# TensorE's order of the first layer written down: scan steps at fixed places among the dense products

## The chip, the cores and the metric

The kernel runs on one core of one Trainium2 chip. The metric is the device time of one launch in microseconds (us), smaller is better. The core's engines run side by side: TensorE (PE in the profile; its weight loads are PEld), VectorE (DVE), ScalarE (ACT), GpSimd (POOL) and SyncE (SP), which here issues nearly all DMAs. Each engine has its own list of instructions, works through it in order, and waits on semaphores where an input or a buffer isn't ready.

## The reference

A two-layer encoder trunk on x of shape (1, 512, 1024), float32. The first layer, the one that the change touches, is a Mamba-2 mixer:

```python
zxbcdt = rms_norm(x, norm_g) @ w_in                  # z 2048, x 2048, B 1024, C 1024, dt 32
xbc = silu(causal_depthwise_conv(xbc, conv_w, conv_b))
y = ssd_chunked_scan(xs * dt, a * dt, bm, cm)        # 8 groups of 4 heads of 64, state 128
y = gated_group_rms_norm(y + d_skip * xs, z, gate_norm_g)
x = x + y @ w_out
```

Of one chunk the scan computes, with `cb = C B^T` within the chunk, `y = (cb * decay) xdt + (C state) exp(acs)` and `state' = state exp(acs_end) + B^T (xdt to_end)`. The second layer is differential attention against one shared K/V projection, and a final RMSNorm follows. Both are outside the change.

## The kernel before

**Dense products.** Every large matrix is used as a high part and a low part (`whi`, `wlo` for weights, made on ScalarE and VectorE from the loaded `raw`), and a product of two such pairs is three TensorE products of 128x512 in a row (`mm3`); three such products are called a triple here. The dense work of the first layer is cut into items that run in the order `z0 g0 g1 z1 g2 g3 z2 g4 o0 g5 z3 g6 g7 o1 o2 o3`: `z` is a quarter of the gate's projection, `g` the projection of one group's B, C and x, `o` a quarter of the output projection (which needs the finished y of two groups). Each item is 32 triples, `o3` here 16 (its other half is done by `last_rows`). A generator, `stream_a`, yields after each triple. `z0` is done ahead of it.

**Scan steps.** When the dense products of group g are traced, `ssd(g)` traces that group's scan, whose TensorE parts are small float32 products and transposes. In the words of the trace and the code: `pcb` (C B^T), `pbt` (transpose of B), `pxt` (transpose of x, two halves), `psA` and `psB` (what the chunks add to the state, L605 to L613), `pyd` (products inside the chunks, 64 small ones, L618 to L625), `po1` and `po2` (C times the state, L633 to L637; `po<-hst` in the trace), and `pyt` (transposes of the normed y). Between them the other engines work: ScalarE copies the first state out of `psA` (L607), GpSimd decays it (L608), and VectorE adds the second half of `psA` to it (L609, `hst<-psA` in the trace). This addition is the last reader of `psA`.

**Buffers.** The eight PSUM banks go by tag: four `mm` for dense products, three `ss`, one `long`. Of a group the `ss` tiles are taken in the order pbt, pxt, pxt, psA, psB, pyd half 0, po1, po2, pyt, pyt. While `psA`, `psB` and `pyd` half 0 are held, none is left, and `po1` takes the bank of whichever is given back first.

**What sets the order.** The program is traced through Tile, which reorders: when the program is built, a list scheduler plays it against a timing model (`schedule_with_timeline_sim=True`) and so fixes each engine's list. An instruction traced earlier has the higher priority; the weights' splitting and the last group's `ssd(7)` have a raised one. `Ordered` wraps the engines: while its `on` is set, an instruction is pinned behind the one traced before it on that engine. In the first layer it is set on TensorE from `psA` to `pyd` (L604 to L626); all else there is where the scheduler's model put it. In `o3` the low and high parts of y of groups 6 (inner steps k = 0, 1) and 7 (k = 2, 3) are used. The splitting of the weights for `last_rows` is pinned on VectorE behind `root_end`, the last instruction of the latest reciprocal root (L273).

Of the kernel before, what the change touches and what calls it, by code (L numbers as in the profile page):

```python
# [13 lines left out]
ALU = mybir.AluOpType  # L14
# [6 lines left out]
NT = S // P  # L21
KD = D // P
G = 8
# [13 lines left out]
BLOCKS = [(it, k) for it in ORDER_B if it[0] not in "bc" for k in range(2 if it[0] == "v" else 1)]  # L37


C_GA, C_GK, C_GB, C_GG, C_SG, C_DTB, C_AL, C_CB, C_CW = 0, 8, 16, 24, 40, 41, 42, 43, 75  # L40
N_PAR = 203

# [3 lines left out]
class Ordered:  # L46


    def __init__(self, tc, engine):
        self.tc, self.engine, self.on = tc, engine, False  # L50

    def __getattr__(self, name):
        op = getattr(self.engine, name)

        def call(*args, **kw):
            i = op(*args, **kw)  # L56
            if self.on:
                self.tc.keep_in_program_order(i)
            return i

        return call
# [3 lines left out]
def trunk(ctx, tc, x, x_t, par, w_dt, w_in, w_out, w_kvqg, w_bo, d_skip, lam_qk, fin_g, out):  # L65
    nc = tc.nc
    V, A, T = (Ordered(tc, e) for e in (nc.vector, nc.scalar, nc.tensor))
# [8 lines left out]
    def mm_bank(name):  # L76
        return psum.tile([P, 512], F32, tag="mm", name=name, bufs=4)
# [4 lines left out]
    def ss_bank(name):  # L82
        turns[0] += 1
        tag = "mm" if turns[0] % turns[1] >= 3 else "ss"
        return psum.tile([P, 512], F32, tag=tag, name=name, bufs=3 if tag == "ss" else 4)

    def long_bank(name):
        return psum.tile([P, 512], F32, tag="long", name=name)
# [13 lines left out]
    x_tok = res.tile([P, NT, D], F32, name="x_tok")  # L102
# [142 lines left out]
    def mm3(ps, lhs, rhs, first, last, **kw):  # L245
        (lh, ll), (rh, rl) = lhs, rhs
        T.matmul(ps, lhsT=lh, rhs=rh, start=first, stop=False, **kw)
        T.matmul(ps, lhsT=lh, rhs=rl, start=False, stop=False, **kw)
        T.matmul(ps, lhsT=ll, rhs=rh, start=False, stop=last, **kw)

    root_end = [None]

    def rsqrt(v, n, tag, bufs=2):


        y = small.tile([P, n], F32, tag=f"{tag}_y", name=f"{tag}_y", bufs=bufs)
        c = small.tile([P, n], F32, tag=f"{tag}_c", name=f"{tag}_c", bufs=bufs)
        iy = small.tile([P, n], I32, tag=f"{tag}_i", name=f"{tag}_i", bufs=bufs)

        def vyy():  # L260
            if n == 1:
                V.scalar_tensor_tensor(out=c, in0=y, scalar=v, in1=y, op0=ALU.mult, op1=ALU.mult)
            else:
                V.tensor_tensor(out=c, in0=y, in1=v, op=ALU.mult)
                V.tensor_tensor(out=c, in0=c, in1=y, op=ALU.mult)

        V.tensor_scalar(out=iy, in0=v.bitcast(I32), scalar1=1, scalar2=None, op0=ALU.logical_shift_right)
        V.tensor_scalar(out=y.bitcast(I32), in0=iy, scalar1=-1.0, scalar2=float(0x5F3759DF - 2 ** 31), op0=ALU.mult, op1=ALU.add)
        vyy()
        V.scalar_tensor_tensor(out=c, in0=c, scalar=-10.0 / 3.0, in1=c, op0=ALU.add, op1=ALU.mult)  # L270
        V.scalar_tensor_tensor(out=y, in0=c, scalar=5.0, in1=y, op0=ALU.add, op1=ALU.mult)
        vyy()
        root_end[0] = V.scalar_tensor_tensor(out=y, in0=c, scalar=-64.0 / 3.0, in1=y, op0=ALU.add, op1=ALU.mult)  # L273
        return y
# [20 lines left out]
    dense = [None]  # L295
# [5 lines left out]
    def until(key):  # L301
        while key not in done:
            next(dense[0], None)
# [76 lines left out]
    xt = [bp2.tile([P, 2, S], F32, tag="yl", name=f"xt{i}", bufs=4) for i in range(4)]  # L380
# [136 lines left out]
                    outs.append(conv(pg[i], *fts[i]))  # L517
        conv_out[g] = outs

    def out_mm(po, j, t, w):  # L520
        tk = slice(t * P, (t + 1) * P)
        for k in range(4):
            yh, yl = yT[2 * j + k // 2]
            mm3(po, (yh[:, k % 2, tk], yl[:, k % 2, tk]), (w[0][:, k, :], w[1][:, k, :]), k == 0, k == 3)
            yield

    def out_proj(j):
        for n in range(2 if j < 3 else 1):
            w = (use if j < 3 else use_b)(("o", j, n))
            ns = slice(n * 512, (n + 1) * 512)  # L530
            for t in range(NT):
                po = mm_bank(f"po{j}_{n}_{t}")
                yield from out_mm(po, j, t, w)
                V.tensor_tensor(out=x_tok[:, t, ns], in0=po, in1=x_tok[:, t, ns], op=ALU.add)
                if j == 3:
                    sq = small.tile([P, S], F32, tag="wide", name=f"sq3_{t}", bufs=2)
                    A.activation(sq, x_tok[:, t, ns], AF.Square, accum_out=bss[:, 0, t:t + 1])

    def stream_a():
        for it in order_a[1:]:  # L540
            j = int(it[1])
            yield from {"z": z_proj, "g": group_proj, "o": out_proj}[it[0]](j)
            done.add(it)
        while True:
            yield

    bss = small.tile([P, 2, NT], F32, name="bss", bufs=1)
    decs = {}
# [20 lines left out]
    def ssd(g):  # L569
        bc, cc, x0, x1 = conv_out.pop(g)  # L570
        xc = (x0, x1)
        dec, een, _ = decs.pop(g)
        hs = slice(R * g, R * g + R)

        pcb = long_bank(f"pcb{g}")
        for c in range(NQ):
            cs = slice(c * P, (c + 1) * P)
            T.matmul(pcb[:, cs], lhsT=bc[:, cs], rhs=cc[:, cs], start=True, stop=True)
        pbt = ss_bank(f"pbt{g}")
        for c in range(3):  # L580
            T.transpose(pbt[:, c * P:(c + 1) * P], bc[:, c * P:(c + 1) * P], ident)
        bt = bp.tile([P, 3, P], F32, tag="bt", name=f"bt{g}")
        A.copy(bt.rearrange("p c n -> p (c n)"), pbt[:, 0:3 * P])
        xdt = bp.tile([P, NQ, R, HD], F32, tag="xdt", name=f"xdt{g}")
        dx = bp.tile([P, NQ, R, HD], F32, tag="dx", name=f"dx{g}")
        for j in range(2):
            pxt = ss_bank(f"pxt{g}_{j}")
            for c in range(NQ):
                T.transpose(pxt[:, c * P:(c + 1) * P], xc[j][:, c * P:(c + 1) * P], ident)
            pv = pxt.rearrange("p (c h e) -> p c h e", h=2, e=HD)  # L590
            h2 = slice(R * g + 2 * j, R * g + 2 * j + 2)
            V.tensor_tensor(out=xdt[:, :, 2 * j:2 * j + 2, :], in0=pv, in1=dt_tok[:, :, h2].unsqueeze(3).to_broadcast([P, NQ, 2, HD]), op=ALU.mult)
            V.tensor_tensor(out=dx[:, :, 2 * j:2 * j + 2, :], in0=pv,
                            in1=dsk[:, h2].unsqueeze(1).unsqueeze(3).to_broadcast([P, NQ, 2, HD]), op=ALU.mult)
# [6 lines left out]
        hst = bp.tile([P, 3, R, HD], F32, tag="hst", name=f"hst{g}")  # L601
        hsf = hst.rearrange("p c h e -> p c (h e)")
        psA = ss_bank(f"psA{g}")
        T.on = True  # L604
        for c in range(2):  # L605
            T.matmul(psA[:, c * 256:(c + 1) * 256], lhsT=bt[:, c, :], rhs=xe[:, c].rearrange("p h e -> p (h e)"), start=True, stop=True)
        A.copy(hsf[:, 0], psA[:, 0:256])  # L607
# [11 lines left out]
        for q in (1, 0):  # L619
            for c in (2 * q, 2 * q + 1):  # L620
                for h in reversed(range(R)):
                    o = (c % 2) * 256 + h * HD

                    for r in (slice(0, 64), slice(64, 128)):
                        T.matmul(pyd[q][r, o:o + HD], lhsT=dec[:, h, c, r], rhs=xdt[:, c, h, :], start=True, stop=True)  # L625
        T.on = False  # L626
        for q in range(2):
            dq = dx[:, 2 * q:2 * q + 2].rearrange("p c h e -> p c (h e)")
            V.tensor_tensor(out=dq, in0=pyd[q].rearrange("p (c e) -> p c e", c=2), in1=dq, op=ALU.add)
# [2 lines left out]

        po1 = ss_bank(f"po1{g}")  # L633
        T.matmul(po1[:, 256:512], lhsT=cc[:, P:2 * P], rhs=hsf[:, 0], start=True, stop=True)
        po2 = ss_bank(f"po2{g}")
        for c in (2, 3):
            T.matmul(po2[:, (c - 2) * 256:(c - 1) * 256], lhsT=cc[:, c * P:(c + 1) * P], rhs=hsf[:, c - 1], start=True, stop=True)  # L637
        V.tensor_tensor(out=tmp[:, 1], in0=po1[:, 256:512].rearrange("p (h e) -> p h e", e=HD),
                        in1=eacs_tok[:, 1, hs].unsqueeze(2).to_broadcast([P, R, HD]), op=ALU.mult)
        V.tensor_tensor(out=tmp[:, 2:4], in0=po2.rearrange("p (c h e) -> p c h e", h=R, e=HD),  # L640
                        in1=eacs_tok[:, 2:4, hs].unsqueeze(3).to_broadcast([P, 2, R, HD]), op=ALU.mult)
        u = dx.rearrange("p c h e -> p c (h e)")
        tm = tmp.rearrange("p c h e -> p c (h e)")
# [7 lines left out]
        r4 = rsqrt(v4, NQ, "y")  # L651
        for c in range(NQ):
            if g == G - 1 and c % 2:
                V.tensor_scalar(out=tm[:, c], in0=u[:, c], scalar1=r4[:, c:c + 1], scalar2=None, op0=ALU.mult)
            else:
                A.activation(tm[:, c], u[:, c], AF.Copy, scale=r4[:, c:c + 1])
        yh = bp2.tile([P, 2, S], F32R, tag="yh", name=f"yh{g}", bufs=4)
# [2 lines left out]

        n = 2 if g == G - 1 else NQ
        for j, a in [(j, a) for a in range(0, NQ, n) for j in range(2)]:
            for c in range(a, a + n):
                T.transpose(pyt[j][:, c * P:(c + 1) * P], tm[:, c, j * P:(j + 1) * P], ident)
            cs = slice(a * P, (a + n) * P)
            A.copy(yh[:, j, cs], pyt[j][:, cs])
            V.tensor_tensor(out=yl[:, j, cs], in0=pyt[j][:, cs], in1=yh[:, j, cs].bitcast(F32), op=ALU.subtract)
        yT[g] = (yh, yl)

    decays((0, 1))  # L670
    dense[0] = stream_a()
    for g in range(G):
        until(f"g{g}")
        if g < G - 1:
            ssd(g)
        else:
            with tc.high_priority():
                ssd(g)
    until("o3")


    hh, hl = new_h("b")
# [27 lines left out]
    due = [0.0]  # L710
# [98 lines left out]
    st = {}  # L809
# [157 lines left out]
    def half(t, n):  # L967
        hs = slice(n * 512, (n + 1) * 512)
        return x_tok[:, t, hs], fg[:, hs], ot[t][:, hs], out[t * P:(t + 1) * P, hs]
# [123 lines left out]
    y, f, o, dst = half(3, 0)  # L1093
# [8 lines left out]
    y, f, o, dst = half(3, 1)  # L1102
# [68 lines left out]
```

## Time and profile before

| | |
|---|---|
| median of 3 runs | 708.0 us (707.85 to 708.36) |
| profiled execution, its own time | 707.88 us |
| its span, first to last instruction | 706.1 us, granted TensorE clock 0.997 |
| busy: PE / PEld / DVE / ACT / POOL | 696.0 / 580.3 / 516.9 / 426.5 / 111.8 us |
| first layer's part touched by the change | about 45 us to 410 us of the span |

How to read it: a row of the timeline has start and duration in us, engine, line, operation, output and inputs by the program's names, shape and count; a bracket at its end is idle time of the engine ahead of it and who ended it. Nearly every instruction goes through the wrapper and so stands under L56, hence groups are told apart by tiles. TensorE products are pipelined: a product of 128x512 is shown as 0.39 us long, but the next one starts about 0.23 us after it, so start-to-start times are what counts.

### The profile page before, as it was taken

To read this page: it belongs to the slowest core of one execution; us is meant where nothing else is said; L and a number is where in the kernel's file an instruction comes from. 1 tells how busy PE (TensorE), PEld (TensorE's weight loads), DVE (VectorE), ACT (ScalarE), POOL (GpSimd) and SP (SyncE) were. 2 spreads that over 40 slices of the span, in tenths; PEclk is the share of its full clock that TensorE was granted. 3 is DMA by queue.
4 is the path that set the end of the run, shared out by engine and by line. 5 is a ranking of instruction groups with operands and counts; after the bars stand their busy time and mean duration, and the time that the engine had idled before them with its cause. 6 is when DMAs were issued, how large, how long until landed. Compare 5 with 4: busy or idle time off the path is not lost.

```text
span 706.1 us, 10493 instructions
## 1 busy us (share of the span) xinstructions
PE 696.0 (99%) x3838; PEld 580.3 (82%) x3838; DVE 516.9 (73%) x1181; ACT 426.5 (60%) x931; POOL 111.8 (16%) x158
## 2 busy tenths in 40 slices
PE   8999999999999999999999999999999999999996
PEld 7887888888888888888888878888888888888884
DVE  5479964889579569568996846467778657787786
ACT  6839672764744637537535357467777567665556
POOL 0009421502406024041110101000000000000002
PEclk9999999999999999999999999999999999999998
DMA  8644313333133331331222311313112221113003
GB/s 297 253 152 151 120 59 126 114 120 120 60 119 120 120 120 60 119 121 59 68 91 82 120 60 54 133 60 119 61 60 84 84 73 60 60 65 115 31 1 119
DMA packets 13491, 70.85 MB, mean 100 GB/s; under 512 B 1792, under 2 KB 3328, under 8 KB 6016
## 3 DMA queue, kind: packets, MB, share of 16 engines
q1 hardware_dynamic: 13008, 69.90, 27.5%
q8 instruction: 30, 0.49, 0.3%
q10 hardware_dynamic: 432, 0.28, 0.1%
q14 instruction: 21, 0.17, 0.1%
HBM read 68.02 MB, written 2.16 MB: 99 GB/s over the span
## 4 chain that ended last, share of the span: by engine, by line
PE 89%; ACT 4%; DVE 3%; DMA 3%; issue 1%; SPq 0%; ACTq 0%; DVEq 0%
PE pg L56 21%; PE po L56 16%; PE pz L56 9%; PE pt L56 8%; PE pq L56 6%; PE pk L56 6%; PE pv L56 6%; PE pb L56 3%; DMA raw<-in_w_in 3%; PE sc L56 3%; PE pyd L56 2%; PE pc L56 2%; ACT whi L56 1%; PE pxt L56 1%; PE psA L56 1%; PE pyt L56 1%
## 5 line engine op out<-in xcount | busy, mean ns | idle before, releaser
L56 DVE SCALAR_TENSOR_TENSOR wlo<-raw,prm,whi 128x512 fp32r<-128x512 f32 (+1 forms) x240 | 148.3, 665 | 56.7 <-ACT whi L56 56.1
L56 ACT ACTIVATE whi<-raw,prm 128x512 fp32r<-128x512 f32 (+1 forms) x240 | 133.6, 628 | 55.5 <-issue 11.0
L56 PE MATMUL pg<-a_hi,whi 128*128 128x512 f32 x256 | 102.2, 399 | 0.1
L56 PE MATMUL pg<-a_lo,whi 128*128 128x512 f32 x256 | 101.1, 395 | 0.0
L56 PE MATMUL pg<-a_hi,wlo 128*128 128x512 f32 x256 | 100.0, 396 | 0.0
L56 DVE SCALAR_TENSOR_TENSOR xc<-pg,prc,xc 128x511 f32<-128x511 f32 (+2 forms) x96 | 70.1, 742 | 7.5 <-ACT xc L56 7.0
L56 PEld LDWEIGHTS pg<-a_hi,whi 128*128 128x128 f32 x256 | 48.1, 188 | 10.2 <-issue 0.7
L56 PEld LDWEIGHTS pg<-a_hi,wlo 128*128 128x128 f32 x256 | 48.1, 188 | 9.8
L56 PEld LDWEIGHTS pg<-a_lo,whi 128*128 128x128 f32 x256 | 48.1, 188 | 9.6
L56 PE MATMUL po<-whi,yh 128*128 128x512 f32 x128 | 50.8, 397 | 0.4 <-ACT yh L56 0.4
L56 PE MATMUL po<-wlo,yh 128*128 128x512 f32 x128 | 50.8, 397 | 0.0
L56 PE MATMUL po<-whi,yl 128*128 128x512 f32 x128 | 50.1, 395 | 0.0
L56 PE MATMUL pz<-wlo,a_hi 128*128 128x512 f32 x128 | 49.3, 394 | 0.0
L56 PE MATMUL pz<-whi,a_hi 128*128 128x512 f32 x128 | 48.8, 395 | 0.4 <-ACT a_hi L56 0.4
L56 PE MATMUL pz<-whi,a_lo 128*128 128x512 f32 x128 | 48.8, 390 | 0.0
L976 POOL TENSOR_TENSOR ot<-x_tok,fg 128x512 f32<-128x512 f32 x4 | 5.0, 1286 | 248.9 <-DVE x_tok L56 248.9
L56 ACT ACTIVATE s<-s,mx 128x128 f32<-128x128 f32 (+3 forms) x64 | 35.6, 557 | 10.2 <-DVE mx L56 10.1
L56 DVE CUSTOM_DVE_ANT_0 s<-sc,bias 128x128 f32<-128x128 f32 (+3 forms) x64 | 29.3, 489 | 15.3 <-PE sc L56 14.8
L56 ACT ACTIVATE xc<-pg,prc 128x512 f32<-128x512 f32 x32 | 24.8, 776 | 24.5 <-DVE pg L56 19.6
L597 POOL TENSOR_TENSOR xe<-xdt,tok 128x256 f32<-128x256 f32 x24 | 14.1, 613 | 161.0 <-DVE xdt L56 161.0
L56 ACT ACTIVATE xc<-xc 128x512 f32<-128x512 f32 x32 | 20.1, 630 | 25.1 <-DVE xc L56 20.2
L561 POOL TENSOR_TENSOR dec<-dec,tok 128x512 f32<-128x512 f32 x32 | 34.9, 1123 | 0.6
(238 smaller groups left out, 1624.6 us busy)
## 6 DMA issues: line engine op xcount, KB each, us to landing
raw<-in_w_in SPq DMA_DIRECT2D x22, 1024.0 KB, 4.9
raw<-in_w_kvqg SPq DMA_DIRECT2D x16, 1024.0 KB, 4.8
dec<-acs_d SPq DMA_DIRECT2D x8, 1024.0 KB, 4.9
raw<-in_w_out SPq DMA_DIRECT2D x8, 1024.0 KB, 4.8
raw<-in_w_bo SPq DMA_DIRECT2D x4, 1024.0 KB, 4.7
x_tok<-in_x SPq DMA_DIRECT2D x4, 512.0 KB, 8.9
out<-ot SPq DMA_DIRECT2D x6, 256.0 KB, 2.1
raw<-in_w_in SPq DMA_DIRECT2D x4, 256.0 KB, 4.9
```

The costliest lines, as they stand in the source:

```text
L56: i = op(*args, **kw)
L561: GP.tensor_tensor(out=dec[:, h], in0=dec[:, h], in1=acs_tok[:, :, R * g + h].unsqueeze(2).to_broadcast([P, NQ, P]), op=ALU.subtract)
L597: GP.tensor_tensor(out=xe[:, c], in0=xdt[:, c], in1=toe_tok[:, c, hs].unsqueeze(2).to_broadcast([P, R, HD]), op=ALU.mult)
L976: GP.tensor_tensor(out=o, in0=y, in1=f, op=ALU.mult)
```

## The change

Every TensorE instruction of the first layer's dense stream and of the scan is written to a log while it is traced, with the name of its step and its group, or None for a dense product. After tracing, `in_places` makes one list: the dense products in traced order, and each step of each group ahead of the dense product that stands the given number of triples (`PLACES`) behind the end of that group's `g` item. Each instruction is pinned behind the one ahead of it in that list. The steps are cb (`pcb`), bt (`pbt`), xt (both `pxt`), st (`psA`, `psB`, `pyd` and `po1`, in one run), o2 (`po2`), yt (`pyt`); the last group has y0 and y2, two chunks each, for yt. The pinning of `psA` to `pyd` by `on` goes away. In `o3` the inner steps 0 and 1 are done for all four row tiles, then 2 and 3 for all four. `root_end` is moved to VectorE's scaling of the last group's y. The number of instructions on each engine stays as it is.

```diff
+PLACES = {
+    "cb": (10, 2, 14, 14, 5, 5, 14, 12),
+    "bt": (3, 24, 21, 44, 35, 25, 21, 37),
+    "xt": (16, 35, 31, 52, 43, 36, 31, 43),
+    "st": (25, 47, 37, 63, 53, 47, 36, 53),
+    "o2": (32, 52, 46, 69, 60, 52, 47, 58),
+    "yt": (56, 85, 76, 99, 89, 85, 69, None),
+    "y0": (None,) * 7 + (69,),
+    "y2": (None,) * 7 + (72,),
+}
...
             if self.on:
                 self.tc.keep_in_program_order(i)
+            elif self.log is not None:
+                self.log.append((self.step, i.ins))
...
-    def out_mm(po, j, t, w):
+    def out_mm(po, j, t, w, ks=range(4)):
         tk = slice(t * P, (t + 1) * P)
-        for k in range(4):
+        for k in ks:
...
-            for t in range(NT):
-                po = mm_bank(f"po{j}_{n}_{t}")
-                yield from out_mm(po, j, t, w)
-                V.tensor_tensor(out=x_tok[:, t, ns], in0=po, in1=x_tok[:, t, ns], op=ALU.add)
+            po = {}
+            for t, ks in [(t, range(4)) for t in range(NT)] if j < 3 else [(t, ks) for ks in ((0, 1), (2, 3)) for t in range(NT)]:
+                if t not in po:
+                    po[t] = mm_bank(f"po{j}_{n}_{t}")
+                yield from out_mm(po[t], j, t, w, ks)
+                if ks[-1] < 3:
+                    continue
+                V.tensor_tensor(out=x_tok[:, t, ns], in0=po[t], in1=x_tok[:, t, ns], op=ALU.add)
...
+            ends[it] = sum(step is None for step, i in T.log)
...
+    def in_places(log):
+
+        dense = [i for step, i in log if step is None]
+        parts = {}
+        for step, i in log:
+            if step:
+                parts.setdefault(step, []).append(i)
+        due = sorted((ends[f"g{g}"] + 3 * PLACES[kind][g], n, kind, g) for n, (kind, g) in enumerate(parts))
+        order = []
+        for n, i in enumerate(dense + [None]):
+            while due and due[0][0] <= n:
+                order += parts[due.pop(0)[2:]]
+            order.append(i)
+        order.pop()
+        assert not due
+        for i, before in zip(order[1:], order):
+            tc.add_manual_dep(i, before.name, mybir.DependencyInfo(mybir.DependencyClass.NoSync, mybir.DependencyReason.DATA), reason="order")
...
         psA = ss_bank(f"psA{g}")
-        T.on = True
+        T.step = "st", g
...
                         T.matmul(pyd[q][r, o:o + HD], lhsT=dec[:, h, c, r], rhs=xdt[:, c, h, :], start=True, stop=True)
-        T.on = False
...
         T.matmul(po1[:, 256:512], lhsT=cc[:, P:2 * P], rhs=hsf[:, 0], start=True, stop=True)
+        T.step = "o2", g
...
             if g == G - 1 and c % 2:
-                V.tensor_scalar(out=tm[:, c], in0=u[:, c], scalar1=r4[:, c:c + 1], scalar2=None, op0=ALU.mult)
+                root_end[0] = V.tensor_scalar(out=tm[:, c], in0=u[:, c], scalar1=r4[:, c:c + 1], scalar2=None, op0=ALU.mult)
...
+            T.step = f"y{a}" if g == G - 1 else "yt", g
...
     until("o3")
+    in_places(T.log)
+    T.log = None
```

More of the change, by code (lines that the diff above doesn't have):

```diff
@@ L50, in __init__ @@
         self.tc, self.engine, self.on = tc, engine, False
+        self.step, self.log = None, None
     def __getattr__(self, name):
@@ L543, in stream_a @@
             done.add(it)
+            ends[it] = sum(step is None for step, i in T.log)
         while True:
             yield
+    ends = {}
+    def in_places(log):
[14 more added lines that the diff above has]
+            tc.add_manual_dep(i, before.name, mybir.DependencyInfo(mybir.DependencyClass.NoSync, mybir.DependencyReason.DATA), reason="order")
     bss = small.tile([P, 2, NT], F32, name="bss", bufs=1)
@@ L573, in ssd @@
         hs = slice(R * g, R * g + R)
+        T.step = "cb", g
         pcb = long_bank(f"pcb{g}")
@@ L578, in ssd @@
             T.matmul(pcb[:, cs], lhsT=bc[:, cs], rhs=cc[:, cs], start=True, stop=True)
+        T.step = "bt", g
         pbt = ss_bank(f"pbt{g}")
@@ L585, in ssd @@
         dx = bp.tile([P, NQ, R, HD], F32, tag="dx", name=f"dx{g}")
+        T.step = "xt", g
         for j in range(2):
@@ L668, in ssd @@
         yT[g] = (yh, yl)
+        T.step = None
     decays((0, 1))
     dense[0] = stream_a()
+    T.log = []
     for g in range(G):
```

## The prediction

> **What bounds the kernel now.** I read the page first: busy shares and the chain of work that ended last.
>
> ```profile
> span 706.1 us, 10493 instructions
> ...
> PE 696.0 (99%) x3838; PEld 580.3 (82%) x3838; DVE 516.9 (73%) x1181; ACT 426.5 (60%) x931; POOL 111.8 (16%) x158
> ...
> PE 89%; ACT 4%; DVE 3%; DMA 3%; issue 1%; SPq 0%; ACTq 0%; DVEq 0%
> ```
>
> TensorE sets the time, so in the first layer a microsecond counts only if TensorE stands still or if an instruction gets a longer start-to-start time. The waits of TensorE alone say how much standing there is:
>
> ```profile
> PE pxt L56 <- ACT xc L56: 1.4, 1, 1.4
> ...
> PE po L56 <- ACT yh L56: 0.4, 1, 0.4
> ```
>
> In the touched part there are only these two. What can be won by another order is therefore small; what can be lost isn't bounded by this view, for the order before is one in which a step that isn't ready is passed by dense products. The chain in order of time gives the price of a dense product and of a run of eight transposes, and where two of the runs `st` stood:
>
> ```profile
> 109.96 0.87 PE pxt L56 x8
> ...
> 127.27 17.96 PE pg L56 x79
> ...
> 160.28 2.95 PE pz L56 x13
> ...
> 344.38 2.73 PE po L56 x12
> ```
>
> A dense product is 17.96 / 79 = 0.227 us, a triple 0.68. The 13 products are those between the end of g3 (32 triples behind g2) and group 2's `psA`: it stood at 36 1/3, and the table says 37, two products later. The 12 are those between the end of g7 and group 6's `psA`: it stood at 36, and the table says 36. Counted in this way nearly every step stood within a triple of its new place, so the dense stream around the steps hardly changes. Three things do: `pxt` of group 0, the end of the last group, and where `po1` goes.
>
> **The change part by part.**
>
> *Runs instead of scattered pieces: 0.* The timeline of TensorE shows two `psA` pieces with one dense product between them:
>
> ```profile
> 388.13 0.60 PE L56 MATMUL psA<-xe,bt 128*128 128x256 f32 x2
> 388.38 0.58 PE L56 MATMUL po<-whi,yl 128*128 128x512 f32 x1
> 388.80 0.59 PE L56 MATMUL psA<-xe,bt 128*128 128x256 f32 x2
> ```
>
> Piece and product take 0.67 together, 0.44 without the 0.23 of the product. Group 2 has `psA` and `psB` as one run (below, 163.07 to 164.46): 1.39 for three pieces, 0.46 each. Gathering saves nothing.
>
> *`xt` of group 0, from 13 to 16 triples: -1.5.*
>
> ```profile
> 63.25 0.39 PE L56 MATMUL pg<-a_lo,whi 128*128 128x512 f32 x1
> ...
> 64.31 1.15 ACT L56 ACTIVATE xc<-xc 128x512 f32<-128x512 f32 x2
> ...
> 65.00 0.66 PE L56 MATMUL pxt<-ident,xc 128*128 128x128 f32 x4 [1.36 <-ACT xc L56]
> ...
> 65.41 0.48 PE L56 MATMUL pg<-a_hi,wlo 128*128 128x512 f32 x1
> ```
>
> From the last product to the first transpose there are 1.75 us instead of 0.23: a wait of 1.52 for the two SiLUs, which end at 65.46. With nine more dense products ahead, the transposes come at 63.48 + 9 x 0.227 = 65.53, just behind both. If ScalarE were 0.5 late, 0.5 of the 1.5 would stay.
>
> *The last group's y and `o3`: -0.5.*
>
> ```profile
> 403.21 2.08 DVE L56 SCALAR_TENSOR_TENSOR wlo<-raw,prm,whi 128x512 fp32r<-128x512 f32 x3
> ...
> 403.46 0.89 ACT L56 ACTIVATE tmp<-dx,y_y 128x256 f32<-128x256 f32 x2
> ...
> 405.21 0.61 DVE L56 TENSOR_SCALAR tmp<-dx,y_y 128x256 f32<-128x256 f32 x2
> ...
> 406.19 0.60 PE L56 MATMUL pyt<-ident,tmp 128*128 128x128 f32 x4
> ...
> 407.14 0.50 PE L56 MATMUL po<-whi,yh 128*128 128x512 f32 x1 [0.35 <-ACT yh L56]
> ```
>
> Behind four transposes the next product came after 0.95 us, against 0.41 at 65.00: 0.54 of wait, because `yh` was copied with no dense work as cover. VectorE scaled its chunks at 405.21, behind three weight splits that began at 403.21. `root_end` moves these splits behind the scaling, so y is ready by about 403.2 + 0.6 for VectorE's chunks and 404.35 for ScalarE's. `y0` at 69 comes nine products earlier, 406.19 - 2.05 = 404.14, when its chunks 0 and 1 are there; the nine products that follow hide the copies. The splits shift by 0.6, and what needs them, `last_rows`, begins only behind all of `o3`; if it didn't, these 0.6 would be lost there. Bounds: 0 to -0.9, if the other two short runs of transposes also get cheaper.
>
> *`po1` goes directly behind `pyd`: this is the price.* It needs ScalarE's copy of the state, and a bank: of the three `ss` banks `psA`, `psB` and `pyd` hold all, and the first to come back is `psA`, when VectorE has added it (`hst<-psA`). In groups 1, 5 and 7 `po1` already stood there without a wait. Group 1:
>
> ```profile
> 120.79 0.42 DVE L56 TENSOR_TENSOR hst<-psA,hst 128x256 f32<-128x256 f32 x1 [6.95 <-POOL hst L608]
> ...
> 122.26 0.70 PE L56 MATMUL po<-hst,xc 128*128 128x256 f32 x2
> ```
>
> VectorE had been idle for 6.95 us, and the addition was over a microsecond ahead of `po1`. Groups 2 and 6 are different. All engines in order of time, group 2:
>
> ```profile
> 163.07 1.03 PE L56 MATMUL psA<-xe,bt 128*128 128x256 f32 x4
> ...
> 164.46 2.08 PE L56 MATMUL pyd<-xdt,dec 128*64 128x64 f32 x64
> ...
> 164.82 0.61 POOL L608 TENSOR_TENSOR hst<-hst,dec 128x256 f32<-128x256 f32 x1 [1.17 <-ACT hst L56]
> ...
> 167.24 1.39 DVE L56 SCALAR_TENSOR_TENSOR xc<-pg,prc,xc 128x510 f32<-128x510 f32 x2
> 168.55 0.41 DVE L56 TENSOR_TENSOR hst<-psA,hst 128x256 f32<-128x256 f32 x1
> ...
> 172.75 0.59 PE L56 MATMUL po<-hst,xc 128*128 128x256 f32 x2
> ```
>
> and group 6:
>
> ```profile
> 346.94 1.03 PE L56 MATMUL psA<-xe,bt 128*128 128x256 f32 x4
> ...
> 348.44 2.08 PE L56 MATMUL pyd<-xdt,dec 128*64 128x64 f32 x64
> ...
> 348.93 0.62 POOL L608 TENSOR_TENSOR hst<-hst,dec 128x256 f32<-128x256 f32 x1 [1.17 <-ACT hst L56]
> ...
> 350.45 0.50 PE L56 MATMUL po<-whi,yh 128*128 128x512 f32 x1
> ...
> 351.94 1.39 DVE L56 SCALAR_TENSOR_TENSOR xc<-pg,prc,xc 128x510 f32<-128x510 f32 x2
> 353.25 0.41 DVE L56 TENSOR_TENSOR hst<-psA,hst 128x256 f32<-128x256 f32 x1
> ...
> 356.02 0.59 PE L56 MATMUL po<-hst,xc 128*128 128x256 f32 x2
> ```
>
> GpSimd had the addend ready at 165.43 and 349.55, but VectorE's list has weight splits and the next group's convolution (`xc`) ahead of the addition, which ends at 168.96 and 353.66. TensorE spent that time on dense products; `po1` came at 172.75 and 356.02. In the new list every later dense product is queued behind `po1`, and with them whoever waits for these products. Group 6: `psA` stays at 346.94, `pyd` is through at 350.45, so `po1` waits 353.66 - 350.45 = **3.2 us**. Group 2: `psA` at 163.07 + 2 x 0.227 = 163.52; `psA` and `psB` 1.39 and `pyd` 2.01 (348.44 to 350.45) make 3.40; `po1` is reached at 166.92 and waits to 168.96, **2.0 us**. Nothing wins this back, since TensorE has no other idle time.
>
> Group 0, VectorE alone:
>
> ```profile
> 70.37 1.57 DVE L56 SCALAR_TENSOR_TENSOR wlo<-raw,prm,whi 128x512 fp32r<-128x512 f32 x2 [0.88 <-ACT whi L56]
> ...
> 76.48 0.42 DVE L56 TENSOR_TENSOR hst<-psA,hst 128x256 f32<-128x256 f32 x1
> ```
>
> From 70.37 VectorE runs without a gap up to the addition, and what it began with waited for ScalarE, not for TensorE. So the 1.5 us won at `xt` don't bring the addition forward. TensorE: 65.53 + 0.87 for the transposes + 27 x 0.227 = 72.53 for `psA`, + 3.40 = 75.93; the addition ends at 76.90: **1.0 us**. Groups 3 and 4 had `po1` 3 products behind `pyd`, with the addition done ahead of `pyd`'s end: 0.
>
> No trace shows `po1` waiting, so bounds: below, 0 for each of the three, if VectorE's new list has the addition first; above, one more convolution instruction in front, 1.39 / 2 = 0.7 each. I take the rows as they stand, since what VectorE has in front of the addition comes from dense products ahead of `st`, and these are unchanged.
>
> Sum: -1.5 - 0.5 + 1.0 + 2.0 + 3.2 = **+4.2 us**. The profiled execution took 707.9, 1.8 more than its span; 707.9 + 4.2 = 712.1, and its distance to the median of 708.0 is 0.1. No DMA is in a moved step; the loads on SP that follow `pyd` or a weight's last use come at most 3.2 us later together with their users.
>
> **The rivals.**
>
> *B, the additions are moved up: 705.9.* VectorE's list is planned anew. If the planner, seeing TensorE held at `po1`, had the addition ahead of the convolutions, or gave `po1` another bank, the waits would be gone and 708.0 - 2.0 remains. For it: the addition was ready 0.9 us ahead of `pyd`'s end in group 6 (349.55 against 350.45), and is traced ahead of those convolutions. Against it: that was so before as well, and they were put first.
>
> *C, one of the two stays: about 709.* For it: group 2's run is shifted by two products, group 6's not at all. 708.0 - 2.0 + 3.2 = 709.2; with group 2's alone 708.0.
>
> *D, the wait costs clock too: about 714.*
>
> ```profile
> 700.00:706.00 6.00, 0.00 (x0) 0.00 (x0) 2.49 (x9) 1.87 (x5) 0.00 (x0) 0.70 0.65 231
> ```
>
> In this stretch without TensorE work the granted clock is 0.70 on the mean: 0.3 x 6 = 1.8 us of clock are lost. Should a wait of 3.2 us bring a fall of that size, 712.1 + 1.8 = 713.9; one more instruction ahead of each addition gives the same. Against it: 3.2 is about half of that stretch. The Trainium skill ("TensorE: Matmul & The Clock Gate", section "Part 1: The HAM clock gate (the "warmup" mystery)") says that an idle window of some 3.4 us halves the clock until about as long a window of work has passed. The trace agrees that idle time lowers it (0.70); by the rule 3.2 us would just not suffice, and a slightly longer wait would cost, as an estimate from that page, 1.7 us.
>
> **How the numbers follow.** About 0.2%, 1.4 us, is what a measurement of this kernel tells from no change. My forecast (710.5 to 713.3) has 0.50, D 0.15, B 0.22, C 0.13. Slower is the forecast and D, 0.65; the same is C, 0.13; faster is B, 0.22. The time is that of the likeliest, 712.1. The range goes from just under B, 705.5, to just over D, 714.2.
>
> **What would show it.** In the waits of TensorE: `pxt` gone, `po` from `hst` new, with VectorE's `hst` as releaser, two long ones near 167 and 350 of 2 and 3 us, one of 1 near 75; nothing at `yh`. The start-to-start time of dense products stays at 0.227. The prediction is wrong if VectorE's list has `hst<-psA` ahead of the convolution instructions in groups 2 and 6, if `po1` finds a bank without it, or if another step (`xt`, `cb`) comes ahead of its input at its fixed place.

## The result, and the profile after

The kernel after takes **727.5 us** (median of 6 runs, 724.8 to 732.9), the kernel before 707.9 beside it (6 runs, 707.7 to 709.0): a ratio of 1.029, 95% interval 1.025 to 1.033. The direction was forecast, the size was not: 4 us were expected and nearly 20 came, far outside the range.

The page of the profiled execution (726.88 us): span, busy times, granted clock in fortieths of the span, and the chain that ended last by engine.

```profile
span 725.1 us, 10491 instructions
...
PE 701.9 (97%) x3838; PEld 583.4 (80%) x3838; DVE 522.2 (72%) x1181; ACT 427.1 (59%) x931; POOL 115.7 (16%) x158
...
PEclk9999999989999999999999999999999999999999
...
PE 72%; DVE 11%; issue 7%; DMA 3%; ACT 3%; POOL 2%; SPq 0%; ACTq 0%; POOLq 0%
```

The span is 19 us longer, but TensorE's busy time only 5.9 (696.0 before). So most of the loss is standing still, and part of it is work that got slower. VectorE, which had 3% of the chain, has 11%. Where TensorE stands is told by its waits (total, times, longest):

```profile
PE pg L68 <- DVE y_c L68: 5.6, 2, 2.8
PE po L68 <- DVE hst L68: 3.2, 3, 1.5
PE pz L68 <- DVE y_i L68: 2.5, 1, 2.5
PE pz L68 <- DVE xc L68: 2.2, 1, 2.2
...
PE pg L68 <- DVE xc L68: 1.3, 2, 0.8
```

Only the second row was forecast. The other four, 11.6 us, are waits of *dense* products, and before there was none of this kind. The longest of them, TensorE, VectorE and ScalarE in order of time:

```profile
147.47 0.39 PE L68 MATMUL pg<-a_hi,wlo 128*128 128x512 f32 x1
...
148.16 0.75 DVE L68 SCALAR_TENSOR_TENSOR xc<-pg,prc,xc 128x511 f32<-128x511 f32 x1 [1.37 <-ACT xc L68]
...
149.73 0.75 DVE L68 SCALAR_TENSOR_TENSOR xc<-pg,prc,xc 128x509 f32<-128x509 f32 x1
150.40 0.15 DVE L68 TENSOR_TENSOR y_c<-y_y,v 128x4 f32<-128x4 f32 x1
...
150.63 0.77 PE L68 MATMUL pg<-a_hi,whi 128*128 128x512 f32 x1 [2.77 <-DVE y_c L68]
```

The product at 150.63 is the first of g3's fourth tile. It takes the PSUM bank that g2's fourth tile had, and the convolution of that tile works in the bank itself; its last reader there is the `xc` at 149.73, which ends at 150.48. The tiny `y_c` named as releaser is only the last VectorE event ahead of the product, and has nothing to do with it. Between the product at 147.47 and this one lie 3.16 us instead of 0.227.

Start to start, six dense products came late in this way, at 58.78, 63.20, 94.13, 147.47, 287.22 and 342.16 (the start of the product ahead), by 0.68, 0.91, 2.39, 2.93, 2.68 and 2.94: **12.5 us** in sum. They open the third and the fourth tile of g1 and the fourth of z1, g3, z3 and g7.

The windows around two of these waits (busy times by engine, then the granted clock, the DMA share and GB/s):

```profile
147.86:149.86 2.00, 0.00 (x0) 0.00 (x0) 1.70 (x5) 0.79 (x2) 0.00 (x0) 1.00 0.82 319
149.86:156.69 6.83, 6.06 (x18) 5.21 (x19) 3.08 (x11) 2.33 (x5) 0.00 (x0) 0.50 0.15 61
...
289.81:293.22 3.41, 3.08 (x7) 2.48 (x8) 1.55 (x10) 3.14 (x6) 0.00 (x0) 0.50 0.02 5
```

TensorE is empty for 2.00 us, then the granted clock falls to 0.50 and stays there for 6.83 us, and later once more for 3.41. Dense products then start 0.43 us apart (151.19, 151.62) instead of 0.227. Of these stretches TensorE works 6.06 and 3.08 us at half the clock; half of that, (6.06 + 3.08) / 2 = **4.6 us**, is lost. In the fortieths of the page it can hardly be seen.

What was forecast can be read as well. `po1` (here `po<-hst`) behind VectorE's addition in groups 0, 2 and 6:

```profile
79.07 0.70 PE L68 MATMUL po<-hst,xc 128*128 128x256 f32 x2 [1.38 <-DVE hst L68]
...
177.38 0.70 PE L68 MATMUL po<-hst,xc 128*128 128x256 f32 x2 [0.27 <-DVE hst L68]
...
369.38 0.41 DVE L68 TENSOR_TENSOR hst<-psA,hst 128x256 f32<-128x256 f32 x1
...
369.84 0.70 PE L68 MATMUL po<-hst,xc 128*128 128x256 f32 x2 [1.55 <-DVE hst L68]
```

From the start of `pyd` to `po1` there are 3.47, 2.35 and 3.63 us in place of 2.01: with a tenth in group 4, **3.5 us**. The two gains are there: neither `pxt` nor `po <- yh` stands in the waits any more. The account of the profiled execution: 12.5 + 4.6 + 3.5 - 2.0 = 18.6, of 726.88 - 707.88 = 19.0. All of it lies ahead of the first `btp` of the second layer (440.52 against 421.58, later by 18.94).

### The profile page after: what moved, and what is told of

Same layout as the page of the kernel before. It is cut to its first block, busy times and chain, and to the rows that moved or that the text cites. A ratio compares the mean times of both kernels' runs of the same rounds, so it can differ in the third digit from the quotient of the medians.

```text
span 725.1 us, 10491 instructions
## 1 busy us (share of the span) xinstructions
PE 701.9 (97%) x3838; PEld 583.4 (80%) x3838; DVE 522.2 (72%) x1181; ACT 427.1 (59%) x931; POOL 115.7 (16%) x158
## 4 chain that ended last, share of the span: by engine, by line
PE 72%; DVE 11%; issue 7%; DMA 3%; ACT 3%; POOL 2%; SPq 0%; ACTq 0%; POOLq 0%
PE po L68 15%; PE pg L68 11%; PE pt L68 7%; PE pz L68 7%; PE pq L68 6%; PE pk L68 6%; PE pv L68 6%; DVE xc L68 4%; PE pc L68 3%; PE pb L68 3%; PE sc L68 3%; DVE wlo L68 3%; DVE dx L68 1%; DMA x_tok<-in_x 1%; PE pyd L68 1%
## 5 line engine op out<-in xcount | busy, mean ns | idle before, releaser
L68 PE MATMUL pg<-a_hi,whi 128*128 128x512 f32 x256 | 104.3, 408 | 6.9 <-DVE y_c L68 5.6
L68 PE MATMUL pz<-whi,a_hi 128*128 128x512 f32 x128 | 50.9, 407 | 5.2 <-DVE y_i L68 2.5
```

## The order of the dense products, looked at again

The prediction counted how many dense products stood ahead of each step, not which. The order in which they were planned, of g3 (number of products in a row into each of its four banks):

```
before: pg0 x12  pg1 x12  pg0 x2 pg1 x2 pg0 x3 pg1 x3  pg2 x12  pg0 x3  pg3 x12  pg0 x4 pg1 x7 pg2 x12 pg3 x12
after:  pg0 x12  pg1 x12  pg2 x12  pg3 x12  pg0 x12  pg1 x12  pg2 x12  pg3 x12
```

Before, the planner opened a new tile later, and in the meantime went on with the second half of tiles whose banks it had. It did so in six items (g1, z1, g3, z2, z3, g7), for 274 of 1344 products. The log is made while the program is traced, and so the written order is the traced one: this rearrangement is gone. The timeline before the change shows a trace of it at the two `x2`: in a triple the operands run `a_hi,whi`, `a_lo,whi`, `a_hi,wlo`, and here one is left after two products for another bank.

```profile
140.76 0.39 PE L56 MATMUL pg<-a_hi,whi 128*128 128x512 f32 x1
140.98 0.39 PE L56 MATMUL pg<-a_lo,whi 128*128 128x512 f32 x1
141.21 0.39 PE L56 MATMUL pg<-a_hi,whi 128*128 128x512 f32 x1
```

**Theory A**: the loss is the traced order of the dense products, which runs into banks still being read, and the clock that falls in the longer waits. **Theory B**: it is the fixed places of the steps, above all `po1`, and the dense order matters little.

## Experiments: dense order and step places apart

**The order of before, steps at their places (e1).** The kernel after, with the dense products of the six items in the planner's order (a table of 45 stretches).

```diff
         dense = [i for step, i in log if step is None]
+        dense[:1344] = [dense[a + k] for a, n in DENSE for k in range(n)]
```

> Theory A (dense products in traced order wait for PSUM banks that the convolution still holds, 12.6 us, and the idle time lowers the clock, some 5 us): with the dense products of the six reordered items put back into the order of the kernel before, and every step still at its place of PLACES, these 17 to 18 us go; the waits of po1 stay or grow from 3.4 to the 6.2 first forecast, so 709 to 713 us. Theory B (the fixed places and po1 themselves cost the time, the order of the dense products does not matter): 724 to 731 us.

714.8 us (713.9 to 717.3), ratio 1.010 (1.009 to 1.012): 12.7 us of the loss are gone with nothing but the order of dense products. The expectation, up to 713, was missed by 1.8 us. TensorE's longest waits in this kernel, but for the start-up:

```profile
PE po L75 <- DVE hst L75: 4.6, 3, 3.2
...
PE pg L75 <- DVE xc L75: 1.2, 2, 1.0
PE pz L75 <- DVE xc L75: 1.2, 1, 1.2
```

Behind the first row stands VectorE's addition again, and the longest of its waits, VectorE and TensorE in order of time, is group 6's:

```profile
357.03 0.41 DVE L75 TENSOR_TENSOR hst<-psA,hst 128x256 f32<-128x256 f32 x1
...
357.49 1.22 PE L75 MATMUL po<-hst,xc 128*128 128x256 f32 x2 [3.20 <-DVE hst L75]
```

The windows of the idle time ahead of it and of the work behind it, with the granted clock behind POOL's busy time:

```profile
354.30:356.77 2.47, 0.00 (x0) 0.00 (x0) 2.47 (x5) 0.00 (x0) 0.00 (x0) 1.00 0.02 3
356.77:363.60 6.83, 6.11 (x14) 4.80 (x15) 5.25 (x11) 2.21 (x6) 1.35 (x2) 0.50 0.42 154
```

From `pyd` to `po1` the three groups lose 1.19, 0.32 and 3.28 us, and the last of these waits brings the clock down, as rival D said: 6.11 us of work at 0.50, 3.1 us lost. A few dense products still wait for a bank, 3.3 us start to start, the longest 1.31 at 164.68; the expectation had nothing for these. The account of the profiled execution, which took 717.33, is 4.8 + 3.1 + 3.3 - 2.0 = 9.2, of 9.5. That the median is only 2.7 us above the forecast of 712.1 is luck, for 3.3 us of bank waits are in it and the wait of group 2 is not. Three of the other executions took 713.9 to 714.8, with granted clocks of 0.996 and 0.997 against 0.993: the clock doesn't fall as far each time.

**The written dense order alone (e2).** The dense products are pinned in traced order, the steps are left to the planner (`psA` to `pyd` pinned in a row as before).

```diff
-        order = []
...
-            order.append(i)
-        order.pop()
-        assert not due
+        order = dense
...
+        T.on = True
...
+        T.on = False
```

> The dense products are pinned to their traced order, the scan steps are left to the planner and psA to pyd pinned as in the kernel before. Theory A: 12.6 us of waits for banks and up to 5 us of lowered clock, no wait of po1: 720 to 727 us. Theory B: as the kernel before, 706 to 709 us.

725.9 us (725.1 to 727.0), ratio 1.025 (1.024 to 1.027): no step has a fixed place, and nearly all of the loss is there. Not all of it is dense products waiting for banks, 9.5 us of idle time in this kernel. `pxt`, which the change frees from its wait, waits again, and against the expectation `po1` waits too, and so does `psA` (from this kernel's waits of TensorE):

```profile
PE pg L68 <- DVE y_c L68: 4.4, 2, 2.5
PE pxt L68 <- ACT xc L68: 1.8, 1, 1.8
...
PE psA L68 <- POOL xe L633: 1.3, 2, 1.0
PE po L68 <- DVE hst L68: 1.2, 1, 1.2
```

**`po1` as a step of its own (e3)**, behind its addition, at the places that it had before the change (rounded to triples).

```diff
+    "o1": (26, 47, 45, 64, 54, 47, 44, 53),
...
+        T.step = "o1", g
         po1 = ss_bank(f"po1{g}")
```

> The changed kernel with po1 as a step of its own at the places it had in the kernel before (26, 47, 45, 64, 54, 47, 44, 53). Theory A: only the 3.4 us of its waits go, 721 to 727 us, with the waits of dense products for banks unchanged. Theory B: most of the loss goes, 706 to 712 us.

726.1 us (724.2 to 727.2), ratio 1.025 (1.024 to 1.027). The waits of `po1` are down to 0.5 us in all, and yet only 1.4 us are won, less than the spread of the kernel after. The longest waits of TensorE in this kernel:

```profile
PE pg L69 <- DVE y_c L69: 5.6, 2, 2.8
PE pz L69 <- DVE xc L69: 3.0, 1, 3.0
PE pz L69 <- DVE y_i L69: 2.3, 1, 2.3
```

The dense waits were expected unchanged, but grew (14.6 us, start to start). Likely the time that TensorE no longer spends at `po1` is time that VectorE no longer has to free banks; no run shows it by itself. With e1, e2 and e3 Theory B falls.

**Both edits together (e4).**

> Both: dense products in the order of the kernel before and po1 as a step of its own. Theory A: no waits left beyond the kernel before, and the two small gains (xt of group 0, the last group's y, 2 us together) remain: 705 to 708 us. Theory B: 720 us or more, since all other steps are still at fixed places.

709.0 us (eleven runs, ten from 708.7 to 710.5, one 716.3), ratio 1.003 (1.001 to 1.004). In the profiled execution no `po1` waits and the clock doesn't fall, and the loss is all but gone. The execution of 716.3 has a granted clock of 0.992 against 0.998 or 0.999 in the ten others, so there it fell once more. But the expectation, up to 708, is missed by a microsecond: the planner's order was made for the planner's step places, and with the steps in whole triples a few dense products still wait, 3.6 us start to start in the profiled execution, more than the 2.0 us of gains. TensorE's longest waits in this kernel:

```profile
PE pz L76 <- DVE xc L76: 1.2, 1, 1.2
PE pg L76 <- DVE xc L76: 0.8, 1, 0.8
PE pg L76 <- ACT zs L76: 0.7, 1, 0.7
```

## Experiments: the clock, and a single swap

**Work inside the waits (e7).** This tells apart what the waits cost and what the clock costs that falls in them. The kernel after, with ten products of zeros ahead of the opening product of the fourth tile of z1, g3, z3 and g7; they add zero to a bank that is being filled, so no sum changes. (The block of zeros is 64 columns wide, for one of 128 finds no room in the on-chip memory beside this kernel's buffers.)

```diff
+    "fl": (None, 12, 12, None, None, 12, 12, None),
...
+    def fill(g, bank):
+        T.step = "fl", g
+        for _ in range(10):
+            T.matmul(bank[0:64], lhsT=zero, rhs=hh[:, 0, :], start=False, stop=False)
+        T.step = None
...
+                if b == 0 and t == 3 and j in (1, 3):
+                    fill({1: 1, 3: 5}[j], pz[2])
...
+                if b == 0 and i == 3 and g in (3, 7):
+                    fill(g - 1, pg[2])
```

> The kernel after, with ten products of a block of zeros (added to a bank that is being filled anyway, so the sums stay the same) ahead of the first product of the fourth tile of z1, g3, z3 and g7, the four places where that product waited 2.4 to 2.9 us for its bank. Ten products are 2.3 us, less than each wait, so they run inside it. If a part of the loss is the clock that falls in such a wait, no fall is left in the first layer, the bank waits themselves stay, and the time is about 5 us below the kernel after: 720 to 724. If the waits alone are the loss and the half clock costs nothing beside them, it stays at 726 to 729. If the fills don't fit into the waits, 40 x 0.227 = 9 us are added: 733 or more.

722.9 us (722.0 to 724.2), ratio 1.021 (1.019 to 1.023): 4.6 us less than the kernel after, with 40 products more. TensorE's timeline of this kernel at g3's fourth tile:

```profile
149.89 2.47 PE L69 MATMUL pg<-a_hi,zero 128*64 128x512 f32 x10
152.83 0.47 PE L69 MATMUL pg<-a_hi,whi 128*128 128x512 f32 x1 [0.47 <-DVE y_c L69]
```

And one window over the whole first layer, with the granted clock:

```profile
25.00:430.00 405.00, 397.54 (x2340) 326.61 (x2339) 303.48 (x551) 217.63 (x386) 107.10 (x140) 1.00 0.28 103
```

The awaited product still comes late, but TensorE's clock is granted whole all the way. The difference of 4.6 us agrees with the 4.6 worked out above from the half-clock stretches, to the tenth only by luck: the medians aren't that sharp, and the profiled executions differ by 2.6, since in this one two more products of g3 wait for a bank (0.69 and 1.30 us at 142.05 and 145.54). The granted clocks of all executions say the same in another way. (1 - granted clock) x span is 2.9 to 12.4 us in the six of the kernel after, and 0.7 to 2.2 in the four with the fills. Taken off the times, it leaves 718.6 to 721.9 and 720.8 to 723.5. So in the profiled execution the clock is about a quarter of the loss, the waits themselves most of the rest.

**One swap in place of the planner's table (e8).** The kernel after with `po1` as its own step, and in the six items the first tile's second half (12 products, 2.73 us) ahead of the fourth tile's first half.

```diff
+    def turn(it):
+        late = it in ("g1", "z1", "g3", "z2", "z3", "g7")
+        return [(0, 0), (0, 1), (0, 2), (1, 0), (0, 3), (1, 1), (1, 2), (1, 3)] if late else [(b, t) for b in range(2) for t in range(4)]
...
-        for b in range(2):
-            wh, wl = use(("g", g, b))
-            for i in range(4):
+        w = {}
+        for b, i in turn(f"g{g}"):
+            if b not in w:
+                w[b] = use(("g", g, b))
```

> The kernel after with po1 as a step of its own (as in e3, 726.1) and one swap in the traced order of six items (g1, z1, g3, z2, z3, g7): the first tile's second half (12 products, 2.73 us) ahead of the fourth tile's first half. No table of the planner's order is used. If the loss is the fourth tile's first product waiting for its bank, 2.73 us of other products cover waits of 0.9 to 2.9 us nearly whole, the long gaps between dense products go and no clock falls: 708 to 712. If it takes the whole of the planner's order, or if the fixed places of the steps cost the time, it stays above 720.

**708.3 us** (eleven runs, 707.7 to 709.6), ratio 1.000 (0.9995 to 1.0013). One swap takes away 18 us of e3's 726.1, and no table is needed. Its waits (the first row is in the start-up, ahead of the first `pg`):

```profile
PE aps_r L69 <- POOL adiag L337: 1.7, 1, 1.7
...
PE pz L69 <- ACT a_hi L69: 0.8, 1, 0.8
PE pg L69 <- DVE xc L69: 0.7, 2, 0.4
PE pz L69 <- DVE xc L69: 0.4, 1, 0.4
```

Of the bank waits 1.1 us are left. It also shows that with the steps at fixed places, and `po1` out of the run, nearly all of the loss is gone. This kernel has both gains of the change in it and still isn't below the kernel before. One reason is seen: start to start the bank waits that are left take 1.5 of the 2.0 us, and from the first `pg` to the first `btp` the profiled execution took 390.3 us against 390.9. Another is not settled: there the first `pg` came at 32.53 (before: 30.65), and one execution can't tell whether that late start belongs to the kernel.

## Experiments: the gains without the written order

**The order of `o3` and the splits behind the scaling, in the kernel before (e5).**

```diff
-    def out_mm(po, j, t, w):
+    def out_mm(po, j, t, w, ks=range(4)):
...
-                V.tensor_scalar(out=tm[:, c], in0=u[:, c], scalar1=r4[:, c:c + 1], scalar2=None, op0=ALU.mult)
+                root_end[0] = V.tensor_scalar(out=tm[:, c], in0=u[:, c], scalar1=r4[:, c:c + 1], scalar2=None, op0=ALU.mult)
```

> The kernel before with two pieces of the change alone: o3's inner steps 0 and 1 for all four row tiles ahead of 2 and 3, and the weight splits of the last rows pinned behind the scaling of the last group's y. The planner is free. The prediction's term for the end of the last group is -0.5 us, so 707.4 where that holds; 707.9 if the order of o3 makes no difference with a planner that could already choose it.

707.7 us (707.5 to 708.2), before 708.0 beside it; ratio 0.9997 (0.9988 to 1.0006). Too small to be told from nothing, and inconclusive between -0.5 and 0.

**The same, and one pin at `xt` of group 0 (e6).**

```diff
+        if g == 1:
+            tc.add_manual_dep(T.late, T.log[136].name, mybir.DependencyInfo(mybir.DependencyClass.NoSync, mybir.DependencyReason.DATA), reason="order")
```

(`T.late` is the first `pxt` transpose of group 0, `T.log[136]` the dense product that the planner had 16 triples behind the end of g0.)

> e5 and one pin more: the first transpose of x of group 0 not before the dense product that stands 16 triples behind the end of g0 (it was 13); everything else is free. If the prediction's two gains (-1.5 and -0.5 us) can be had without the written order, 705.9 to 706.5. If the pin makes psA of group 0 late and the planner's new list waits elsewhere for it, 707 to 708.5.

**706.5 us** (eleven runs, 705.7 to 707.7), ratio 0.998 (0.997 to 0.999): below both kernels, 1.5 us under the 708.0 beside it. All waits of TensorE behind the start-up's:

```profile
PE pz L57 <- ACT a_hi L57: 0.4, 1, 0.4
PE po L57 <- ACT yh L57: 0.2, 1, 0.2
PE pg L57 <- ACT zs L57: 0.2, 1, 0.2
```

`pxt` is gone from the list and no wait of a like size has taken its place. What the change could win is had with e5's edits and one dependency, which alone is worth 1.2 us (706.5 against 707.7); the other pins are not needed for it.

## Why the prediction was wrong

**The step that failed** is the sentence "so the dense stream around the steps hardly changes", under what bounds the kernel now: the sum has no term for the dense products' own order. Its own sign, "The start-to-start time of dense products stays at 0.227", is the one that failed, six times by 0.68 to 2.94 us. The rows behind the sentence, `pg` x79 and the like, count products, and a count doesn't show which they are: the rows don't give buffer numbers. The text even said that before, a step that isn't ready is passed by dense products, but it did not ask what passes a *dense product* that isn't ready. It was the planner's second use of the same freedom, and in the profiled execution it was worth 12.5 us of waits and 4.6 of clock.

**The waits of `po1`** were rightly found, and with the dense order of before (e1) rightly priced for group 0 (1.0 forecast; 1.19) and group 6 (3.2; 3.28). Group 2 was forecast at 2.0 and cost 0.32. That is not rival B: between VectorE's last multiplication in a `pg` bank and the addition stand four weight splits and three convolution instructions, as before (5.21 us against 5.57). TensorE came later. The dense product behind 164.68, ahead of `psA`, waits 1.31 us for its bank, and `psA` stands two products further back (0.45); VectorE works on meanwhile, and so the addition starts 1.9 us behind `pyd`'s start in place of 4.1. Most of this wait has moved to a dense product. In the kernel after itself groups 2 and 6 wait only 0.3 and 1.6. There VectorE has one convolution instruction fewer in that stretch, as rival B says in a mild form (group 6: 5.16 us against 6.17). That is 1.0 of the 1.7 us that group 6 waits less; that the dense waits ahead of it let VectorE catch up for the rest is likely, but no run tells it apart.

**The gains.** `xt` of group 0: right. The kernel after has SiLUs and transposes as forecast:

```profile
63.95 1.15 ACT L68 ACTIVATE xc<-xc 128x512 f32<-128x512 f32 x2
...
67.17 1.03 PE L68 MATMUL pxt<-ident,xc 128*128 128x128 f32 x8
```

The transposes come 2 us behind the SiLUs (forecast: just behind, but two late dense products of g1 stand ahead of them), without a wait, and e6 against e5, 1.2 us, is near the 1.5 of the forecast. The last group's -0.5 is not refuted and not shown: the wait of 0.4 is gone in the kernel after, and e5 is 0.25 below before, within its uncertainty. Runs instead of scattered pieces at 0: right, `psA` to `pyd` takes 1.39 us as in group 2 before.

**Rival D** had the right mechanism at a wrong place and price. 1.8 us were taken from the stretch behind the last product; measured were 3.1 at group 6 in e1, and 4.6 at two dense waits in the kernel after. Its argument against itself, that 3.2 us is only half of the stretch of 6, rests on a mean. In finer windows the trace of the kernel before has the fall already 2.53 us behind its last product's end, sooner than 3.2:

```profile
699.84:702.37 2.53, 0.00 (x0) 0.00 (x0) 2.42 (x9) 1.49 (x4) 0.00 (x0) 1.00 0.97 361
702.37:706.00 3.63, 0.00 (x0) 0.00 (x0) 0.23 (x1) 0.51 (x1) 0.00 (x0) 0.50 0.44 145
```

The rule that rival D cites, from the Trainium skill ("TensorE: Matmul & The Clock Gate", section "Part 1: The HAM clock gate (the "warmup" mystery)"), says that it takes an idle window of some 3.4 us, and was used to say that 3.2 us would just not suffice. The measurement differs from it: TensorE was empty for 2.00 and 2.47 us when the clock fell. The same section says that the window is free-running; the falls here, none of them after the same idle time, agree with that.

**The range** had the cases of `po1` at its upper end and one clock fall on top. Nothing in it stood for a change of order of 274 products, which could have been counted without any run, by comparing the traced order with the planned one, bank by bank; the broken triples in the timeline before were a sign of it.

## What to carry to other kernels

Before an order is written down, compare it with the planner's instruction by instruction, by buffer and not by kind: an in-order engine waits at the first product whose bank is still read, while a planner may have been passing it by. If an order is to be fixed, open a new tile only when its bank's last reader is surely done, here by putting 12 products of another tile ahead of it. And when only one wait is to go, one dependency at that place is safer than a full list: it won 1.2 us where the full list lost 20.

## What the runs showed of the hardware

An idle time of TensorE well below 3 us can halve its clock: it fell 2.00 us after the last product's end in the kernel after and 2.47 us after it in e1. It can also fall when the wait is already over: in e2 TensorE was empty for 2.53 us, worked again for 0.49 us at the whole clock, and then worked 3.41 us at half.

```profile
337.36:337.85 0.49, 0.49 (x2) 0.45 (x3) 0.49 (x2) 0.49 (x2) 0.00 (x0) 1.00 0.00 0
337.85:341.26 3.41, 3.41 (x9) 2.65 (x9) 3.41 (x8) 1.56 (x3) 0.00 (x0) 0.50 0.02 5
```

In the first layer of the profiled executions the clock stayed at half for 3.41 us five times (after, e2, e3) and for 6.83 us twice (after, e1), never for another time. Not every wait of that length did it: at 94.13 (2.62 us from start to start) and 342.16 (3.17) in the kernel after the clock stayed whole.

```profile
94.00:97.00 3.00, 0.77 (x4) 0.38 (x3) 2.57 (x5) 2.08 (x2) 0.89 (x2) 1.00 0.39 164
342.00:346.00 4.00, 1.21 (x6) 0.74 (x5) 2.99 (x10) 1.99 (x4) 0.00 (x0) 1.00 0.69 262
```

What decides between them the profile doesn't show, and the time of a kernel with such waits varies with it: the six runs of the kernel after spread over 8 us, with mean granted clocks of 0.985 and 0.983 in the two longest spans (731.1 and 729.2) and 0.996 in the shortest (723.0), while the kernel before spreads over 1.3.
